# Second block's qkv and attention queries by token from split weights, on one Trainium2 core

## The chip, the cores and the metric

The kernel runs on one core of a Trainium2 chip. The metric is the device time of one execution in microseconds (us), as the median of several runs. The engines are TensorE (PE in the profile, with its weight loads as PEld), VectorE (DVE), ScalarE (ACT), GpSimd (POOL) and SyncE (SP, which here only issues transfers). They run side by side, each along its own queue, and wait for each other by semaphores.

## What is computed

The reference chains two transformer blocks on 256 tokens of width 1024. The first mixes tokens with two gated linear attentions and then sends every token through 8 x 16 experts that are gathered by index. The second block has four branches, whose inputs come from one projection `h @ w_in`; what matters here of it:

```python
h = _rmsnorm(x, norm_pre)
cols = h @ w_in
(dn_qkv, dn_z, dn_b, dn_a, gm_uv, gm_z, sw_q, sw_k, sw_v, sw_z,
 xm_q, xm_z, gate_logits) = _split_cols(cols)
mem_kv = _rmsnorm(mem, norm_mem) @ w_mem_kv
y_a = _deltanet_branch(dn_qkv, dn_z, dn_b, dn_a, conv_w, a_log, dt_bias, dn_norm)
y_b = _spatial_gating_branch(gm_uv, gm_z, gm_norm, spatial_w, spatial_b)
y_c = _sliding_window_branch(sw_q, sw_k, sw_v, sw_z, sinks)
y_m = _memory_branch(xm_q, xm_z, mem_kv)
ys = jnp.stack([y_a, y_b, y_c, y_m], axis=2)
proj = jnp.einsum("btnc,ncd->btnd", ys, w_up)
gates = jax.nn.sigmoid(gate_logits.reshape(B, T, N_BRANCH, D))
merged = jnp.sum(gates * proj, axis=2)
out = merged @ w_out
return x + _rmsnorm(out, norm_post)
```

`dn_qkv` (1536 columns) goes through a causal convolution of four taps along the tokens and a silu; `sw_q` and `xm_q` (512 columns each) are the queries of the two attention branches.

## The kernel before

The 256 tokens are two blocks of 128, b = 0 and 1. The weights lie in HBM as tiles of 128 x 1024 (two chunks of 128 rows by 512 columns), and 512 output columns are a group of four tiles. `load_to` (L205) issues the transfers on SP in the order of the stream, `wt` (L231) calls for a chunk of a tile and keeps the loads ahead.

Products are done in two ways. With float32 operands (`proj_chan` in its second branch, L414) the weights are the stationary operand, the result comes out channel by token, and a chip instruction leaves two records. With split operands (`mm3`, L370) a tile is cut into a high part (a cast on ACT, L216) and a low part (a subtraction on DVE, L217), and three products of 128x512 replace one of full precision: `proj_tok` (L377) for one block, `both_tok` (L391) for both. They come out token by channel. `is_split` and `SPLIT` (L53) say which groups are split; `cut_to` (L219) splits tiles up to `state["ahead"]` tiles before their use, into a ring of six pair buffers.

Block 0 of the second block (`pre2`, `small_proj`, `qkv`, `q_proj`, `deltanet`, L1028 to L1317) runs in the shadow of the expert gathers of block 1: `gathers` (L930) hands a step to the side work between two gathers. After the last gather come `last_out(1)`, the two gm groups (`spatial_u`), and then the tail, in which TensorE follows `tail_main` (L1674). It does, for block 1, the small projection (`swk`), the three qkv groups and the two query groups `swq` and `xmq` channel by token from unsplit weights; after them the four z groups (first `zgm`), the gates and the up products for both blocks, from split weights. Into this order `pace` (L89) sets the steps of four side chains: the delta rule (`tail_delta`, with the products gc, gcr, l2p, l2r), the spatial branch (gmv, sp, yb) and the two attentions (own, prev, sws). `pace` goes by a count of steps, not by durations: a step that is set there waits in its engine's queue until what it needs is ready, and everything behind it on that engine waits too.

For each qkv group, ACT copies the result to `qkvr`, DVE puts the last three tokens of block 0 ahead of it, ACT does the first tap and DVE the other three for each of four channel blocks (L1072, L1074), and a tanh on ACT and one DVE step make the silu.

At the end, `merge(3)` (L1485) adds the last up product into `mg`, block by block, `finish_T` turns `mg` (pt) and `finish` does the out product (o) from the last two split groups.

Of the kernel before, what the change touches and what calls it, by code (L numbers as in the profile page):

```python
# [19 lines left out]
P = 128  # L20
# [26 lines left out]

(G_IN, G_V, G_G, G_OUT, G_Q, G_OUT2, G_MEM, G_QKV, G_SWQ, G_XMQ, Z_GU, Z_GV, G_AGAIN, Z_GZ, Z_SW, Z_XM, Z_DN, G_GATE,
 G_O2, G_END) = (0, 3, 5, 7, 9, 12, 15, 17, 20, 21, 22, 23, 24, 29, 30, 31, 32, 33, 45, 47)
AGAIN = G_AGAIN - G_QKV  # L50
STREAM = (*range(12), 7, 8, *range(12, 22), *range(15, 20), *range(22, 40))

SPLIT = ((G_IN, G_Q), (Z_GU, G_AGAIN), (Z_GZ, G_END))  # L53

UP_B, UP_C, UP_M, UP_A = 0, 1, 2, 3

# [85 lines left out]
def kernel(ctx, tc, I, out, dbg=None):  # L142
    nc = tc.nc
    dbg = dbg or {}
    V, S, G, TE = nc.vector, nc.scalar, nc.gpsimd, nc.tensor
# [10 lines left out]
    def slot(name, dt=F32):  # L156

        return big.tile([P, 1024], dt, tag="slot", name=name)

    def slot3(name, n, w=P, dt=F32):  # L160
        return slot(name, dt)[:, :n * w].rearrange("p (a b) -> p a b", b=w)
# [6 lines left out]
    turn = {"at": 0, "ring": N_PAIR}  # L168
# [114 lines left out]
    def bank4(name, tag="ps"):  # L283
        return bank(name, tag).rearrange("p (a b) -> p a b", b=P)
# [92 lines left out]
    def proj_tok(g, xT, name, n=KC, c0=0, w0=0):  # L377

        ps = bank(name)
        for c in range(n):  # L380
            x = xT(c0 + c)
            if isinstance(x, tuple):
                mm3(ps, x, wt2(g, w0 + c), c == 0, c == n - 1)
            else:
                TE.matmul(ps, x, wt(g, w0 + c), start=c == 0, stop=c == n - 1)
                pe(0.9)
            if c % 2:
                yield
        return ps
# [16 lines left out]
    def proj_chan(ps, g, cb, xT):  # L406

        s = slice(cb * P, (cb + 1) * P)
        for c in range(KC):
            x = xT(c)  # L410
            if isinstance(x, tuple):
                mm3(ps, [w[:, s] for w in wt2(g, c)], x, c == 0, c == KC - 1)
            else:
                TE.matmul(ps, wt(g, c)[:, s], x, start=c == 0, stop=c == KC - 1)  # L414
                pe(0.244)
# [610 lines left out]
    B2 = {}  # L1026
# [16 lines left out]
    def h_of(b):  # L1043
        return lambda c: hT[b][:, c]

    def h2_of(b):
        return lambda c: (hh2[b][0][:, c], hh2[b][1][:, c])

    tail3 = {}

    def qkv(b):

        qkvT = []
        for g in range(3):
            ps = bank("qkv")
            for cb in range(4):
                proj_chan(ps[:, cb * P:(cb + 1) * P], G_QKV + b * AGAIN + g, cb, h_of(b))
                yield
            yield
            raw_ = slot("qkvr")[:, :4 * (P + 3)].rearrange("p (a b) -> p a b", a=4)  # L1060
            S.copy(raw_[:, :, 3:], ps.rearrange("p (a b) -> p a b", a=4))
            if b:
                V.tensor_copy(raw_[:, :, :3], tail3[b - 1, g])
            else:
                V.memset(raw_[:, :, :3], 0.0)
            if b + 1 < NB:
                tail3[b, g] = cpool.tile([P, 4, 3], F32, name=f"tail{b}{g}")
                V.tensor_copy(tail3[b, g], raw_[:, :, P:P + 3])
            dst = slot3(f"qkvT{b}{g}", 4)
            for cb in range(4):  # L1070
                cw = chan[:, C_CW + 4 * (4 * g + cb):C_CW + 4 * (4 * g + cb) + 4]
                S.activation(dst[:, cb], raw_[:, cb, 0:P], AF.Copy, scale=cw[:, 0:1])  # L1072
                for tap in range(1, 4):
                    V.scalar_tensor_tensor(dst[:, cb], raw_[:, cb, tap:tap + P], cw[:, tap:tap + 1],  # L1074
                                           dst[:, cb], op0=OP.mult, op1=OP.add)
                if cb % 2:
                    yield
            th = small("th", 512).rearrange("p (a b) -> p a b", b=P)
            S.activation(th, dst, AF.Tanh, scale=0.5)
            V.scalar_tensor_tensor(dst, th, 1.0, dst, op0=OP.add, op1=OP.mult)  # L1080
            qkvT.append(dst)
            yield
        B2["qkvT", b] = qkvT

    def small_proj(b):

# [12 lines left out]
        B2["swk", b], B2["swv", b], B2["ba", b] = k, v, ba  # L1099
        yield  # L1100

    def q_proj(g, name, b):
        dst = slot3(f"{name}{b}", 4)
        ps = bank(name)
        for j in range(4):
            proj_chan(ps[:, j * P:(j + 1) * P], g + b * AGAIN, j, h_of(b))
            yield
        S.copy(dst, ps.rearrange("p (j t) -> p j t", j=4))
        B2[name, b] = dst

    def z_silu(z, name, gain=None):

        t = B2[name, 0] = slot3(f"{name}_t", 2, 512)
        pss = yield from both_tok(z, (h2_of(0), h2_of(1)), name)
        for b, ps in enumerate(pss):
            dst = t[:, b]
            if gain is not None:
                gate_tok(dst.rearrange("p (h d) -> p h d", h=4), ps, gain)
            else:
                th = small("th", 512)  # L1120
                S.activation(th, ps, AF.Tanh, scale=0.5)
                V.tensor_scalar(th, th, 0.5, 0.5, op0=OP.mult, op1=OP.add)
                V.tensor_tensor(out=dst, in0=th, in1=ps, op=OP.mult)
            B2[name, "of", b] = dst
            yield
# [348 lines left out]
    def gate_proj(n):  # L1474
        for b in range(NB):
            gates[b, n] = slot(f"gate{b}{n}")
        for nh in range(2):
            pss = yield from both_tok(G_GATE + 3 * n + nh, (h2_of(0), h2_of(1)), "gate")
            for b, ps in enumerate(pss):
                S.activation(gates[b, n][:, nh * 512:(nh + 1) * 512], ps, AF.Tanh, scale=0.5)  # L1480
            yield
# [37 lines left out]
    def finish_T(b):  # L1519
        fin[b] = slot3(f"mh{b}", 8, P, F32R), slot3(f"ml{b}", 8, P, F32R)  # L1520

        def put(h, pt):
            hi, lo = [t[:, 4 * h:4 * h + 4] for t in fin[b]]
            S.activation(hi, pt, AF.Copy, scale=0.5)
            V.scalar_tensor_tensor(lo, pt, 0.5, hi.bitcast(F32), op0=OP.mult, op1=OP.subtract)

        yield from transposed(mg[b], put)
# [145 lines left out]

    def tail_main():  # L1674
        yield from small_proj(1)
        yield from qkv(1)
        yield from q_proj(G_SWQ, "swq", 1)
        yield from q_proj(G_XMQ, "xmq", 1)
        yield from z_silu(Z_GZ, "zgm")
        yield from z_silu(Z_SW, "zsw")  # L1680
        yield from z_silu(Z_XM, "zxm")
        yield from z_silu(Z_DN, "zdn", gain=rows[:, R_DN:R_DN + P])
        for n in range(3):
            yield from gate_proj(n)
            yield from merge(n)
        yield from gate_proj(3)
        turned, i = finish_T(0), 0
        for waits in merge(3):
            yield waits
            i += waits is not True  # L1690
            if i > 6:
                next(turned, None)
        yield from turned
# [98 lines left out]
```

## Time and profile before

| what | value |
|---|---|
| median of 3 runs | 1202.18 us (1202.08 to 1202.36) |
| the profiled execution, its time and span | 1201.17 us, 1199.4 us |
| TensorE, busy | 1066.5 us (89%) |
| DVE, busy | 869.9 us (73%) |
| ACT, busy | 508.0 us (42%) |
| splits of tiles: casts on ACT (L216), subtractions on DVE (L217) | 108 of 1052 ns, 108 of 1220 ns |
| 512 float32 products of block 0 and 1 for qkv, records | x384, 275 ns median |

The profile is one execution on the chip. A group of its rows is a line of the kernel, an engine, an operation and a tile, with the busy time and the mean of one. In the views in order of time a row has the start and the time in us, the engine, the line, the operation with output<-inputs and their sizes, how many instructions it merges, and in brackets how long the engine stood idle before it and whom it waited for. The granted clock of TensorE (PEclk) is a share of 2.4 GHz. Times are from the start of the span.

### The profile page before, as it was taken

The numbers are of one execution on the slowest core, as the hardware profiler recorded it, in microseconds if no ns is written. First come the engines' busy times: TensorE is split into PE (matmuls) and PEld (weight loads), VectorE is DVE, ScalarE is ACT, GpSimd is POOL, SyncE is SP. The second block draws the span as 40 slices with busy tenths as digits, with TensorE's granted clock in tenths as the row PEclk, the third lists the DMA queues.
The fourth block names the chain that finished last, engine by engine and source line by source line (L and its number), as shares of the span: only waits on it lengthen the run. The fifth ranks groups of instructions, "written<-read, shape, count | busy, mean of one in ns | idle before, by whom it ended". The sixth has DMA issues, their size and how long they took to land.

```text
span 1199.4 us, 14824 instructions
## 1 busy us (share of the span) xinstructions
PE 1066.5 (89%) x4988; PEld 732.5 (61%) x4988; DVE 869.9 (73%) x1872; ACT 508.0 (42%) x1271; POOL 317.1 (26%) x278
## 2 busy tenths in 40 slices
PE   8999979989979885986888898886999999999987
PEld 6887634545437652733655554543469988888876
DVE  5588587887588667979888899974735686456644
ACT  5625333442343342432444644546534444444441
POOL 1000234334434342543433454552200000000000
PEclk9999989899989997997989989999999999999989
DMA  9626599999999999999999999999753843445520
GB/s 364 220 102 225 209 363 367 355 375 391 427 427 425 425 421 426 425 427 426 406 424 425 403 388 427 426 427 427 288 202 141 300 158 127 127 154 190 191 90 36
DMA packets 68075, 376.40 MB, mean 314 GB/s; under 512 B 7696, under 2 KB 8992, under 8 KB 35232
## 3 DMA queue, kind: packets, MB, share of 16 engines
q0 software_dynamic: 36864, 268.45, 54.4%
q1 hardware_dynamic: 29264, 103.56, 24.2%
q10 hardware_dynamic: 1872, 3.44, 0.8%
q8 instruction: 40, 0.66, 0.2%
q14 instruction: 35, 0.29, 0.1%
HBM read 374.38 MB, written 1.05 MB: 313 GB/s over the span
## 4 chain that ended last, share of the span: by engine, by line
PE 46%; DVE 22%; DMA 15%; issue 7%; ACT 6%; POOL 3%; POOLq 0%; SPq 0%; DVEq 0%; ACTq 0%
DMA uv<-in_peer_uv_dram,idx 12%; PE acc L910 10%; DVE uv L887 8%; POOL uv L858 3%; PE pq L414 3%; PE gate L373 2%; PE gate L375 2%; PE gate L374 2%; DMA w<-in_wts_dram 2%; PE qkv L414 2%; DVE x L904 2%; PE lv L620 2%; DVE wp L217 1%; PE up L373 1%; PE up L374 1%
## 5 line engine op out<-in xcount | busy, mean ns | idle before, releaser
L910 PE MATMUL acc<-uv,dg 128*128 128x512 f32 x852 | 432.3, 644 | 98.5 <-ACT dg L898 93.7
L858 POOL DMA_INDIRECT uv<-in_peer_uv_dram,idx x256 | 303.8, 1187 | 429.5 <-PE acc L910 253.1
L887 DVE SCALAR_TENSOR_TENSOR uv<-uv,hn 128x1024 f32<-128x1024 f32 x256 | 307.9, 1220 | 80.5 <-DMA uv<-in_peer_uv_dram,idx 75.8
L910 PEld LDWEIGHTS acc<-uv,dg 128*128 128x128 f32 x852 | 161.4, 204 | 284.9 <-issue 146.2
L891 ACT ACTIVATE ge<-act 128x1 f32<-128x1 f32 x256 | 51.7, 202 | 376.1 <-DVE uv L887 353.6
L217 DVE TENSOR_TENSOR wp<-w,wp 128x1024 fp32r<-128x1024 f32 x108 | 129.2, 1220 | 74.7 <-ACT wp L216 74.6
L216 ACT CAST wp<-w 128x1024 fp32r<-128x1024 f32 x108 | 110.0, 1052 | 53.8 <-PE up L375 17.7
L898 ACT ACTIVATE dg<-mats,wv 128x128 f32<-128x128 f32 x213 | 82.9, 389 | 4.6 <-PE acc L910 3.1
L295 POOL TENSOR_TENSOR rsb<-rsa,mhalf 128x1 f32<-128x1 f32 (+2 forms) x8 | 7.3, 908 | 283.5 <-DVE rsa L292 283.5
L892 ACT ACTIVATE wv<-ge,gw 128x1 f32<-128x1 f32 x256 | 75.4, 295 | 8.3
L414 PEld LDWEIGHTS pq<-hnT,w 128*128 128x128 f32 x512 | 60.5, 192 | 9.0 <-issue 8.8
L414 PE MATMUL pq<-hnT,w 128*128 128x128 f32 x512 | 61.3, 275 | 0.0
L904 DVE SCALAR_TENSOR_TENSOR x<-uv,wv,x 128x1024 f32<-128x1024 f32 x43 | 55.0, 1280 | 1.9 <-ACT wv L892 1.9
L373 PE MATMUL gate<-wp,hh 128*128 128x512 f32 x128 | 51.7, 404 | 0.0
L414 PEld LDWEIGHTS qkv<-hT,w 128*128 128x128 f32 x384 | 46.4, 196 | 6.8 <-issue 6.6
L375 PE MATMUL gate<-wp,hl 128*128 128x512 f32 x128 | 49.9, 390 | 0.0
L374 PE MATMUL gate<-wp,hh 128*128 128x512 f32 x128 | 49.9, 390 | 0.0
L414 PE MATMUL qkv<-hT,w 128*128 128x128 f32 x384 | 46.4, 279 | 0.0
L323 POOL TENSOR_TENSOR rst<-rst,mhalf 128x1 f32<-128x1 f32 x5 | 2.8, 559 | 146.0 <-DVE rst L322 146.0
L1074 DVE SCALAR_TENSOR_TENSOR qkvT<-qkvr,chan,qkvT 128x128 f32<-128x128 f32 x72 | 24.0, 351 | 5.7 <-ACT qkvT L1072 4.0
L375 PEld LDWEIGHTS gate<-wp,hl 128*128 128x128 f32 x128 | 24.0, 188 | 5.2
L891 ACT ACT_TABLE_LOAD x21 | 26.9, 1283 | 0.4
(503 smaller groups left out, 1780.5 us busy)
## 6 DMA issues: line engine op xcount, KB each, us to landing
w<-in_wts_dram SPq DMA_DIRECT2D x188, 512.0 KB, 4.9
uv<-in_peer_uv_dram,idx POOLq DMA_INDIRECT x256
wsm<-in_w_small_dram ACTq DMA_DIRECT2D x8, 132.0 KB, 9.9
x<-in_x_dram SPq DMA_DIRECT2D x2, 512.0 KB
skT<-in_skT_dram ACTq DMA_DIRECT2D x2, 512.0 KB
mem<-in_mem_dram SPq DMA_DIRECT2D x2, 512.0 KB
out_dram<-o SPq DMA_DIRECT2D x4, 256.0 KB
row_n<-in_gains_dram ACTq DMA_DIRECT2D x1, 512.0 KB
```

The source lines that it names most:

```text
L216: S.copy(hi, x)
L217: (eng or V).tensor_tensor(out=lo, in0=x, in1=hi.bitcast(F32), op=OP.subtract)
L373: TE.matmul(ps, fh, sh, start=start, stop=False)
L374: TE.matmul(ps, fh, sl, start=False, stop=False)
L375: TE.matmul(ps, fl, sh, start=False, stop=stop)
L414: TE.matmul(ps, wt(g, c)[:, s], x, start=c == 0, stop=c == KC - 1)
L858: G.indirect_dma_start(out=t, out_offset=None, in_=I["peer_uv"], in_offset=bass.IndirectOffsetOnAxis(ap=idx[b][:, h, s:s + 1], axis=0))
L887: V.scalar_tensor_tensor(t, t, 1.0, hn[b], op0=OP.mult, op1=OP.mult, accum_out=act[:, h, s:s + 1])
L891: S.activation(ge, act[:, h, s:s + 1], AF.Gelu)
L898: S.activation(dg[diags], ident, AF.Copy, scale=wv[diags])
L904: V.scalar_tensor_tensor(xr[b], t, wv[sums], xr[b], op0=OP.mult, op1=OP.add)
L910: TE.matmul(acc[b][:, nh], dg[sums], t[:, nh * 512:(nh + 1) * 512], start=start, stop=h == 7 and s == 15)
```

## The change

The qkv and query groups of block 1 are now split like the groups after them, so all groups from the gm groups to the end are (`SPLIT`). A new driver, `by_channel`, does each group token by channel with `proj_tok`, copies the result to SBUF (ACT, tile `qkvt`, `swqt` or `xmqt`) and turns it with four transposes (pt) after the second tile of the next group; the last one is turned inside zgm. What followed the products (`qkv_of`, `q_of`) then reads the turned tile. Block 0 keeps its float32 products; its `q_proj` hands on one step more. In the last merge, tiles are split two ahead instead of four. The other lines of the file move by -1 up to L1048 and by up to +41 behind.

```diff
-AGAIN = G_AGAIN - G_QKV
...
-SPLIT = ((G_IN, G_Q), (Z_GU, G_AGAIN), (Z_GZ, G_END))
+SPLIT = ((G_IN, G_Q), (Z_GU, G_END))
...
+    def by_channel(groups, last):
+
+
+        def steps(p):
+            for k, waits in enumerate(p):
+                yield waits
+                if k == 1 and turn:
+                    yield from turned(*turn)
+
+        def turned(t, use):
+            pt = bank4("pt")
+            for c in range(4):
+                TE.transpose(pt[:, c], t[:, c * P:(c + 1) * P], ident)
+            yield
+            yield from use(pt)
+
+        def product(g, name):
+            ps = yield from proj_tok(g, h2_of(1), name)
+            products.append(ps)
+
+        turn, products = None, []
+        for g, name, use in groups:
+            yield from steps(product(g, name))
+            t = slot(f"{name}t")[:, :512]
+            S.copy(t, products.pop())
+            turn = t, use
+        yield from steps(last)
+
...
-                proj_chan(ps[:, cb * P:(cb + 1) * P], G_QKV + b * AGAIN + g, cb, h_of(b))
+                proj_chan(ps[:, cb * P:(cb + 1) * P], G_QKV + g, cb, h_of(b))
                 yield
             yield
+            yield from qkv_of(b, g)(ps.rearrange("p (a b) -> p a b", a=4))
+
+    def qkv_of(b, g):
+        def use(ps):
             raw_ = slot("qkvr")[:, :4 * (P + 3)].rearrange("p (a b) -> p a b", a=4)
-            S.copy(raw_[:, :, 3:], ps.rearrange("p (a b) -> p a b", a=4))
+            S.copy(raw_[:, :, 3:], ps)
...
+    def q_of(name, b):
+        def use(ps):
+            dst = slot3(f"{name}{b}", 4)
+            S.copy(dst, ps)
+            B2[name, b] = dst
+            yield
+
+        return use
+
     def q_proj(g, name, b):
-        dst = slot3(f"{name}{b}", 4)
         ps = bank(name)
         for j in range(4):
-            proj_chan(ps[:, j * P:(j + 1) * P], g + b * AGAIN, j, h_of(b))
-            yield
-        S.copy(dst, ps.rearrange("p (j t) -> p j t", j=4))
-        B2[name, b] = dst
+            proj_chan(ps[:, j * P:(j + 1) * P], g, j, h_of(b))
+            yield
+        yield from q_of(name, b)(ps.rearrange("p (j t) -> p j t", j=4))
...
         yield from small_proj(1)
-        yield from qkv(1)
-        yield from q_proj(G_SWQ, "swq", 1)
-        yield from q_proj(G_XMQ, "xmq", 1)
-        yield from z_silu(Z_GZ, "zgm")
+        yield from by_channel([(G_AGAIN + g, "qkv", qkv_of(1, g)) for g in range(3)]
+                              + [(G_AGAIN + 3, "swq", q_of("swq", 1)), (G_AGAIN + 4, "xmq", q_of("xmq", 1))],
+                              z_silu(Z_GZ, "zgm"))
...
         yield from gate_proj(3)
+        state["ahead"] = 2
```

How the queues change shows at three places. The names are those of the tiles with the number of their buffer; wp and a number is a split tile of the stream, 96 to 99 that of qkv group 0, 100 to 103 of group 1, and so on by fours to 112 to 115 of xmq; th, dd and dg_r belong to the silu of a group and to the decay gates.

ACT, before, from the end of the decay gates' first step to the copy of group 1:

```order
L1139 ACTIVATE dg_r_6508<-ba_6496 128x4
L1061 COPY qkvr_6554<-qkv_6510 128x4x128 [waits PE_49]
L1072 ACTIVATE qkvT10_6557<-qkvr_6554,chan_78 128x128 [waits DVE_49]
L1072 ACTIVATE qkvT10_6557<-qkvr_6554,chan_78 128x128 x3
L1079 ACTIVATE th_6584<-qkvT10_6557 128x512 [waits DVE_49]
L1154 ACTIVATE dg_r_6508<-dg_r_6508 128x4 [waits DVE_49]
L1155 ACTIVATE dg_r_6508<-dg_r_6508 128x4 [waits DVE_49]
L1162 ACTIVATE dd_6609<-dd_6609 128x512 [waits DVE_49]
L1163 ACTIVATE dd_6609<-dd_6609 128x512 [waits DVE_49]
L1061 COPY qkvr_6657<-qkv_6587 128x4x128 [waits PE_49]
```

ACT, in the change, behind the copy of group 0 out of PSUM (qkvt) and up to that of group 1:

```order
L215 CAST wp104_6572<-w104_6534 128x1024 [waits DMAHW1_49]
L215 CAST wp105_6586<-w105_6545 128x1024 [waits DMAHW2_49]
L1091 COPY qkvr_6610<-pt_6595 128x4x128 [waits PE_49]
L1102 ACTIVATE qkvT10_6613<-qkvr_6610,chan_78 128x128 [waits DVE_49]
L1102 ACTIVATE qkvT10_6613<-qkvr_6610,chan_78 128x128 x3
...
L1196 ACTIVATE dg_r_6520<-dg_r_6520 128x4 [waits DVE_49]
L1203 ACTIVATE dd_6635<-dd_6635 128x512 [waits DVE_49]
L1204 ACTIVATE dd_6635<-dd_6635 128x512 [waits DVE_49]
L1109 ACTIVATE th_6646<-qkvT10_6613 128x512
L215 CAST wp106_6651<-w106_6556 128x1024 [waits DMAHW3_49]
L215 CAST wp107_6665<-w107_6570 128x1024 [waits DMAHW4_49]
L1074 COPY qkvt_6674<-qkv_6569 128x512 [waits PE_49]
```

Between the first taps of group 0 and the copy of group 1 now stand the decay gates' steps, the tanh of group 0 and the casts of 106 and 107; the copy of group 1 before stood behind the exponentials alone and fed the taps directly.

TensorE, in the change, from the end of tile 104 (group 2) to tile 106; before, the products of group 2 had no operation of their own group between them:

```order
L374 MATMUL qkv_6676<-wp104_6572,hl1_6338 128x512
L1399 MATMUL sp_6688<-gmv_6405,swT_3159 128x128 [waits DVE_49,Activation_49]
L1399 MATMUL sp_6688<-gmv_6405,swT_3159 128x128 x3
L1399 MATMUL sp_6693<-gmv_6405,swT_3159 128x128 [waits DVE_49]
L1399 MATMUL sp_6693<-gmv_6405,swT_3159 128x128 x3
L372 MATMUL qkv_6676<-wp105_6586,hh1_6337 128x512
L373 MATMUL qkv_6676<-wp105_6586,hh1_6337 128x512
L374 MATMUL qkv_6676<-wp105_6586,hl1_6338 128x512
...
L1062 MATMUL pt_6709<-mats_77,qkvt_6674 128x128 [waits DVE_49,Activation_49]
L1062 MATMUL pt_6709<-mats_77,qkvt_6674 128x128 x3
L372 MATMUL qkv_6676<-wp106_6651,hh1_6337 128x512
L373 MATMUL qkv_6676<-wp106_6651,hh1_6337 128x512 [waits DVE_49]
```

The transposes of group 1 stand between the second and the third tile of group 2, and all tiles behind them wait with them.

DVE, before, in the last merge (gate and mg of the two halves of block 0 and the first of block 1):

```order
L217 TENSOR_TENSOR wp180_8397<-w180_8341,wp180_8397 128x1024 [waits DMAHW5_49,PE_49,Activation_49]
L217 TENSOR_TENSOR wp181_8408<-w181_8358,wp181_8408 128x1024 [waits DMAHW6_49,PE_49,Activation_49]
L1498 SCALAR_TENSOR_TENSOR gate03_8249<-gate03_8249,up_8394 128x512 [waits PE_49]
L1499 TENSOR_TENSOR mg0_7661<-mg0_7661,gate03_8249 128x512 [waits DVE_49]
L217 TENSOR_TENSOR wp182_8422<-w182_8375,wp182_8422 128x1024 [waits DMAHW7_49,Activation_49]
L217 TENSOR_TENSOR wp183_8433<-w183_8395,wp183_8433 128x1024 [waits DMAHW0_49,Activation_49]
L1498 SCALAR_TENSOR_TENSOR gate03_8249<-gate03_8249,up_8419 128x512
L1499 TENSOR_TENSOR mg0_7661<-mg0_7661,gate03_8249 128x512 [waits DVE_49]
L1525 SCALAR_TENSOR_TENSOR ml0_8452<-pt_8453,mh0_8451 128x512 [waits Activation_49]
L1498 SCALAR_TENSOR_TENSOR gate13_8250<-gate13_8250,up_8444 128x512
L1499 TENSOR_TENSOR mg1_7663<-mg1_7663,gate13_8250 128x512 [waits DVE_49]
```

and in the change:

```order
L1539 SCALAR_TENSOR_TENSOR gate03_8304<-gate03_8304,up_8449 128x512 [waits PE_49]
L1540 TENSOR_TENSOR mg0_7721<-mg0_7721,gate03_8304 128x512 [waits DVE_49]
L216 TENSOR_TENSOR wp180_8471<-w180_8396,wp180_8471 128x1024 [waits DMAHW5_49,Activation_49]
L216 TENSOR_TENSOR wp181_8482<-w181_8413,wp181_8482 128x1024 [waits DMAHW6_49,Activation_49]
L1539 SCALAR_TENSOR_TENSOR gate03_8304<-gate03_8304,up_8468 128x512 [waits PE_49]
L1540 TENSOR_TENSOR mg0_7721<-mg0_7721,gate03_8304 128x512 [waits DVE_49]
L1566 SCALAR_TENSOR_TENSOR ml0_8501<-pt_8502,mh0_8500 128x512 [waits Activation_49]
L1539 SCALAR_TENSOR_TENSOR gate13_8305<-gate13_8305,up_8493 128x512 [waits PE_49]
L1540 TENSOR_TENSOR mg1_7723<-mg1_7723,gate13_8305 128x512 [waits DVE_49]
L1566 SCALAR_TENSOR_TENSOR ml0_8501<-pt_8515,mh0_8500 128x512 [waits Activation_49]
L1539 SCALAR_TENSOR_TENSOR gate13_8305<-gate13_8305,up_8524 128x512 [waits PE_49]
L1540 TENSOR_TENSOR mg1_7723<-mg1_7723,gate13_8305 128x512 [waits DVE_49]
```

The subtractions of 182 and 183 have moved from ahead of the second half of mg0 to behind both halves of mg1.

## Rows read from the trace of the kernel before

**Rows 1.** Windows: stretch, length, busy PE, PEld, DVE, ACT, POOL, PEclk, DMA, GB/s.

```profile
900.00:920.00 20.00, 20.00 (x170) 19.61 (x170) 6.86 (x24) 9.40 (x20) 1.10 (x2) 1.00 0.30 106
920.00:940.00 20.00, 20.00 (x182) 20.00 (x181) 15.66 (x51) 8.04 (x20) 0.00 (x0) 1.00 0.73 254
940.00:960.00 20.00, 20.00 (x137) 18.16 (x137) 11.45 (x15) 10.59 (x20) 1.65 (x1) 1.00 0.88 305
960.00:980.00 20.00, 19.49 (x112) 16.55 (x111) 17.95 (x31) 10.13 (x21) 0.00 (x0) 1.00 0.54 179
```

**Rows 2.** TensorE in order of time, 891 to 951 us: start, time, operation.

```profile
891.20 0.39 PE L373 MATMUL gm<-wp,hh 128*128 128x512 f32 x1
...
896.64 0.39 PE L373 MATMUL gm<-wp,hh 128*128 128x512 f32 x1
...
905.72 7.31 PE L414 MATMUL qkv<-hT,w 128*128 128x128 f32 x64
912.86 0.28 PE L1146 MATMUL gc<-dg_g,mats 128*128 128x4 f32 x2
...
914.20 7.31 PE L414 MATMUL qkv<-hT,w 128*128 128x128 f32 x64
...
940.99 1.16 PE L1376 MATMUL own<-swk,swq 64*128 64x128 f32 x8
...
942.97 3.84 PE L414 MATMUL xmq<-hT,w 128*128 128x128 f32 x32
...
950.52 0.48 PE L373 MATMUL zgm<-wp,hh 128*128 128x512 f32 x1
```

**Rows 3.** TensorE in order of time, the tail.

```profile
1158.28 0.60 PE L350 MATMUL pt<-mats,mg 128*128 128x128 f32 x4
1158.63 0.48 PE L373 MATMUL up<-wp,yT 128*128 128x512 f32 x1
...
1164.08 1.08 PE L350 MATMUL pt<-mats,mg 128*128 128x128 f32 x4 [3.81 <-DVE mg L1499]
1164.81 0.78 PE L373 MATMUL up<-wp,yT 128*128 128x512 f32 x1
...
1169.91 0.40 PE L373 MATMUL o<-wp,mh 128*128 128x512 f32 x1
```

**Rows 4.** ACT in order of time, 887 to 923 us.

```profile
887.18 3.90 ACT L216 CAST wp<-w 128x1024 fp32r<-128x1024 f32 x4
...
910.89 0.20 ACT L1139 ACTIVATE dg_r<-ba 128x4 f32<-128x4 f32 x1
...
922.67 0.63 ACT L1162 ACTIVATE dd<-dd 128x512 f32<-128x512 f32 x1 [1.67 <-DVE dd L1160]
```

**Rows 5.** DVE in order of time: the last gathers, the stretch, the tail.

```profile
815.35 1.23 DVE L887 SCALAR_TENSOR_TENSOR uv<-uv,hn 128x1024 f32<-128x1024 f32 x1 [1.21 <-DMA uv<-in_peer_uv_dram,idx]
...
888.26 4.63 DVE L217 TENSOR_TENSOR wp<-w,wp 128x1024 fp32r<-128x1024 f32 x4 [0.26 <-ACT wp L216]
903.51 0.15 DVE L292 TENSOR_SCALAR rsa<-ss 128x1 f32<-128x1 f32 x1 [10.63 <-ACT th L316]
...
913.68 0.17 DVE L1063 COPY qkvr<-tail 128x12 f32<-128x12 f32 x1 [2.39 <-ACT qkvr L1061]
...
918.48 1.41 DVE L1354 SCALAR_TENSOR_TENSOR gmv<-gmv,rsb,row_gm 128x512 f32<-128x512 f32 x2
...
920.41 0.15 DVE L1152 COPY dg_r<-gc 128x4 f32<-128x4 f32 x1
...
922.81 0.15 DVE L1165 SCALAR_TENSOR_TENSOR dg_r<-dg_r 128x4 f32<-128x4 f32 x1
...
929.33 2.15 DVE L1362 SCALAR_TENSOR_TENSOR yb<-sp,chan,gmu 128x128 f32<-128x128 f32 x8
...
1159.55 1.22 DVE L217 TENSOR_TENSOR wp<-w,wp 128x1024 fp32r<-128x1024 f32 x1 [2.63 <-ACT wp L216]
```

**Rows 6.** Windows, TensorE alone, in the tail: busy, PEclk, DMA, GB/s.

```profile
1166.00:1170.00 4.00, 4.00 (x12) 0.54 0.00 0
```

More of the change, by code (lines that the diff above doesn't have):

```diff
@@ L1049 @@
     tail3 = {}
+    def by_channel(groups, last):
[20 more added lines that the diff above has]
+        yield from steps(last)
     def qkv(b):
-        qkvT = []
         for g in range(3):
@@ L1080, in qkv @@
             V.scalar_tensor_tensor(dst, th, 1.0, dst, op0=OP.add, op1=OP.mult)
-            qkvT.append(dst)
+            three = B2.setdefault(("qkv", b), [])
+            three.append(dst)
+            if len(three) == 3:
+                B2["qkvT", b] = three
             yield
-        B2["qkvT", b] = qkvT
+        return use
     def small_proj(b):
@@ L1100, in small_proj @@
         yield
+    def q_of(name, b):
[4 more added lines that the diff above has]
+            yield
+        return use
     def q_proj(g, name, b):
-        dst = slot3(f"{name}{b}", 4)
         ps = bank(name)
         for j in range(4):
-            proj_chan(ps[:, j * P:(j + 1) * P], g + b * AGAIN, j, h_of(b))
+            proj_chan(ps[:, j * P:(j + 1) * P], g, j, h_of(b))
             yield
-        S.copy(dst, ps.rearrange("p (j t) -> p j t", j=4))
-        B2[name, b] = dst
+        yield from q_of(name, b)(ps.rearrange("p (j t) -> p j t", j=4))
     def z_silu(z, name, gain=None):
```

## The prediction

> **What bounds the kernel now.** I read the windows first, then the instructions of TensorE, VectorE (DVE) and ScalarE (ACT) in order of time. Between 900 and 960 us TensorE is busy 20.00 us of every 20 at a granted clock of 1.00, while DVE has 6.86, 15.66 and 11.45 us [rows 1]. So the stretch that the change rewrites, from the small projection at 902 us to the first z product at 950.52 us [rows 2], is bound by TensorE, and DVE seems to have room. That room is the question: what counts is not its sum but its place in the queues of DVE and ACT, each of which runs its instructions in the order in which they stand.
>
> **TensorE's part.** A group is now 32 full-precision products of 128x128 (64 records); the first one starts at 905.72 and what follows it at 912.86, 7.14 us [rows 2]. In the change a group is 24 products of 128x512 with split weights; the two token products of gm start at 891.20 and 896.64, so 24 of these take 5.44 us, 1.36 us a tile [rows 2]. Behind each group come four transposes, which in the tail take 0.35 us, with 0.09 us more for the first product behind them [rows 3]: 0.45 us. Five groups go from 35.7 to 29.45 us: 6.25 us less work for TensorE.
>
> **ACT's and DVE's part.** The 20 tiles of these groups have to be split: a cast on ACT, four in 3.90 us, 0.975 us each [rows 4], and a subtraction on DVE, four in 4.63 us, 1.16 us each [rows 5]. That adds 19.5 us to ACT and 23.2 us to DVE, and ACT gets five more copies of 128x512 out of PSUM, at 0.6 us like the other ACT steps of that size (0.63 us [rows 4]). The first four tiles fit into a hole of 10.63 us on DVE before 903.51 [rows 5] and cost nothing. The other sixteen stand among the rest. I walk through them on the clock of the profile before.
>
> Start. ACT has three table loads behind the small projection and is free at 911.1 [rows 4]. Only then come the casts of tiles 100 to 103, done at 912.1 to 915.0; the subtractions of 100 to 104 follow to 917.9, and behind them the two small steps of the decay gates, to 918.3. TensorE ends group 0 at 911.16, does tiles 100 and 101 and the first transposes to 916.2, then stands at the product gc, which needs those small steps: 2.1 us. With gc at 1.34 us (912.86 to 914.20 [rows 2]), tiles 102 to 104, the product sp (sixteen records, as own and prev have together: 1.98 us) and tile 105 it comes to 927.05.
>
> First long wait. Next on TensorE are the transposes of group 1, whose copy stands on ACT behind the casts of 106 and 107, these behind the tanh of group 0 and two exponentials, and these behind DVE's work on group 0. From 918.3: a small step and the subtraction of 105, 1.4; the two gmv products, 1.41; the convolution of a group from its tail copy to its last tap, 4.80 (913.68 to 918.48); the gate differences, 2.40 (920.41 to 922.81) [rows 5]; three ACT steps of about 0.6 [rows 4], 1.7; two casts, 1.95; the copy, 0.6. Sum 14.3: 932.6. TensorE waits 5.5 us.
>
> Second long wait. It then does transposes, tiles 106 to 109 (0.4 us late for one subtraction) and stands at 938.9 before the transposes of group 2. DVE: subtraction 106 ends at 932.2, a small step and two products, 1.6; subtractions 107 to 109, 3.5; the yb products, 2.15; the convolution, 4.80 [rows 5]: 944.2. ACT: tanh 0.6, two casts, the copy: 947.4. TensorE waits 8.5 us.
>
> Third wait. After tiles 110 to 113 TensorE is at 953.3. Subtraction 110 ends at 947.0, 111 to 113 at 950.4, the convolution at 955.2; ACT's tanh and two squares end at 957.0 (l2p can start, 3.7 us late), casts 114 and 115 at 959.0, the copy of swq at 959.6, casts 116 and 117 and the copy of the turned swq at 962.1. Only then come the scores own and prev, 1.98 us (940.99 to 942.97 [rows 2]), tiles 114 and 115, 2.72, and own and prev once more: zgm starts at 968.8 instead of 950.52 [rows 2]. So the stretch costs **18.3 us more**, the 6.25 us of TensorE's saving already in it. Behind 960 us TensorE was busy 19.49 of 20 [rows 1] with the same work as in the change, so nothing takes the delay back.
>
> What of it is not seen in a row: how the queues of DVE and ACT mesh. If all sixteen splits hid, the stretch would gain 6.25 us; if every one of them lay bare on DVE, sixteen times 1.16 us would cost 18.6 us less the 6.25. The chain above comes out beyond the second bound by about 6 us, because ACT and DVE also wait for each other, so I take the chain and use both ends in the cases below. The weights' transfers stay hidden: a raw buffer is now free after the subtraction instead of after the products, and the DMA engines are busy 0.30 to 0.88 of the stretch [rows 1].
>
> **The tail.** With the split-ahead set to 2, the splits of tiles 182 and 183 stand behind the sums of mg0 and mg1. Before, DVE waited for their casts (the first came at 1159.55, after 2.63 us [rows 5]) and added mg0 only behind both; TensorE stood 3.81 us for it and then ran slower: its twelve up products that start at 1164.81 end where the next product starts, at 1169.91, 5.1 us instead of 12 times 0.227 (5.44 / 24) [rows 3]. In that stretch the granted clock was 0.54, its lower level of 1.2 GHz [rows 6]. In the change the second half of mg0 needs only the up half that ends 1.36 us before 1158.28 [rows 3] and two DVE steps on 128x512 (two took 1.41 us [rows 5]), so it is there at about 1159.5, before the transposes are due at 1160.1. From 1160.1 to the out product 9.8 us become 0.36 + 2.72 + 0.1 = 3.2 us: **6.6 us less**. The later splits (182 to 187) are then due at one in 1.36 us, against 0.975 us on ACT and 1.16 on DVE. Bounds: 0, if one of them holds TensorE as mg0 did, and 6.6.
>
> **The gathers.** q_proj hands on one step more in block 0, which moves the side work behind the gathers by one gather. The wait of DVE for a gather in that place was 1.21 us [rows 5]; one gather more or less in front of the ACT-bound end is worth between -1.2 and +2.5 us (one gather and its dot, 1.23 + 1.21). I take **+0.5**.
>
> **Sum.** 18.3 - 6.6 + 0.5 = +12.2 us. The profiled execution took 1201.17 us for a span of 1199.4; the median of the runs is 1202.18, 1.01 above. So 1202.18 + 12.2 = **1214.4 us**.
>
> **Rivals.**
> (1) Faster: TensorE stays the bound. If ACT and DVE stay ahead of it, as the free sums of 13.1, 4.3 and 8.6 us of DVE in the three windows allow on paper [rows 1], both savings come: 1202.18 - 6.25 - 6.6 + 0.5 = 1189.8 us. The Trainium skill's Perfetto Trace Analysis, "Identifying the Most-Contended Engine", says to optimize the engine with the highest occupancy first; by that rule, with TensorE at 20.00 of 20, this is the case to expect. Against it: the copy that feeds the transposes stands behind two casts and the whole convolution of the group before, whatever the sums are. It decides for this case if the copy of group 1 ends before 927 us. Chance 0.08.
> (2) No change: the waits come, but half as long, since the stages mesh better than I add them up. 18.3 would have to shrink to about 6, with the tail's 6.6 against it: 1202.2 us. Chance 0.05.
> (3) Slower than forecast: the clock. After each of the three waits TensorE starts at its lower level, as after the 3.81 us in the tail, where the restart cost 5.1 - 2.72 = 2.4 us, and 0.4 more in the transposes, 1.08 instead of 0.60 [rows 3]. Behind the first and the second wait this lies under the next wait; if it does not, or lasts into zgm, three times 2.7 us come on top: 1222.5 us. The Trainium skill's TensorE: Matmul & The Clock Gate, "HAM oscillation", states that waits between bursts of products bring the clock down each time; by that rule this is the time. The tail's wait agrees (0.54), but no row here shows a wait that another wait follows. Chance 0.10.
> (4) The tail does not do what it says: tile 182 or 186 holds TensorE instead of mg0, and the 6.6 us stay: 1221.0 us. Chance 0.05.
>
> **Numbers.** That leaves 0.72 for the forecast, whose own range is 1207 to 1220: the gathers move it by 2 and each of the three chains by some 2 us. The range 1206 to 1222 takes in case 4 and part of case 3 and leaves out about 2 in 10. A measurement of this kernel tells some 0.2%, 2.4 us, from no change. Slower by more: 0.72 + 0.10 + 0.05 = 0.87; within: 0.05; faster: 0.08.
>
> **What would show it.** In the profile of the changed kernel: zgm starts 17 to 20 us later against the small projection; TensorE has idle times of about 5, 8 and 4 us before the transposes pt of groups 1 and 2 and before l2p, released by ACT copies named qkvt; the granted clock falls between 925 and 965 us; the 3.81 us wait for mg is gone, and from the last gate product to the end there are about 6.6 us less. It would be wrong if the copies qkvt end within a microsecond of their products, if TensorE stays busy through to zgm, or if the tail keeps a wait of over 2 us.

## Result: 1212.8 us, slower by 1%

The changed kernel takes 1212.8 us in the median (1212.25 to 1214.6, 4 runs), the kernel before 1202.13 us (4 runs); the ratio is 1.0097 with a 95% interval of 1.0085 to 1.0109. The forecast was 1214.4 us in a range of 1206 to 1222. The profiled execution of the change has a span of 1211.2 us, 11.8 more than before.

The windows of the changed kernel (the columns are those of [rows 1], to which they answer):

```profile
900.00:920.00 20.00, 16.84 (x92) 13.93 (x92) 11.15 (x23) 14.06 (x25) 1.10 (x2) 1.00 0.52 186
920.00:940.00 20.00, 13.15 (x54) 10.31 (x52) 17.31 (x47) 8.11 (x16) 0.00 (x0) 0.83 0.33 108
940.00:960.00 20.00, 13.98 (x59) 11.62 (x60) 16.34 (x26) 15.23 (x23) 1.32 (x1) 0.70 0.51 162
960.00:980.00 20.00, 20.00 (x97) 16.64 (x97) 9.90 (x14) 8.96 (x25) 1.27 (x1) 0.87 0.51 178
```

TensorE, 20.00 of 20 before, is busy 13 to 14 of 20 from 920 to 960 us, and its granted clock falls to 0.83 and 0.70 in the two windows. TensorE in order of time, the changed kernel (answers to [rows 2]):

```profile
899.03 1.95 PE L1124 MATMUL swk<-hT,wsm 128*128 128x128 f32 x16
...
912.93 0.60 PE L1062 MATMUL pt<-mats,qkvt 128*128 128x128 f32 x4
915.19 0.36 PE L1187 MATMUL gc<-dg_g,mats 128*128 128x4 f32 x2 [1.66 <-DVE dg_r L1184]
...
928.63 1.12 PE L1062 MATMUL pt<-mats,qkvt 128*128 128x128 f32 x4 [3.40 <-ACT qkvt L1074]
...
943.04 1.12 PE L1062 MATMUL pt<-mats,qkvt 128*128 128x128 f32 x4 [5.55 <-ACT qkvt L1074]
...
952.36 1.95 PE L1224 MATMUL l2p<-one,X 128*128 128x1 f32 x16 [0.78 <-ACT X L1219]
...
957.61 2.08 PE L1417 MATMUL own<-swk,swq 64*128 64x128 f32 x8 [1.26 <-ACT swq L1139]
...
968.06 0.50 PE L372 MATMUL zgm<-wp,hh 128*128 128x512 f32 x1
```

The waits stand where the forecast put them, before the transposes of groups 1 and 2, and their releaser is the copy qkvt on ACT. From swk to zgm it is 69.03 us instead of 48.44 (902.08, the start of swk before, to 950.52). That is 20.6 us more, a little beyond the 17 to 20 us that the forecast named as its sign. ACT in order of time shows what the copies stand behind, the tanh of the group before and two casts:

```profile
925.61 0.61 ACT L1109 ACTIVATE th<-qkvT 128x512 f32<-128x512 f32 x1
926.12 1.97 ACT L215 CAST wp<-w 128x1024 fp32r<-128x1024 f32 x2
928.01 0.57 ACT L1074 COPY qkvt<-qkv 128x512 f32<-128x512 f32 x1
...
935.28 1.28 ACT L1102 ACTIVATE qkvT<-qkvr,chan 128x128 f32<-128x128 f32 x4 [4.31 <-DVE qkvr L1093]
939.99 0.63 ACT L1109 ACTIVATE th<-qkvT 128x512 f32<-128x512 f32 x1 [3.43 <-DVE qkvT L1104]
940.53 1.98 ACT L215 CAST wp<-w 128x1024 fp32r<-128x1024 f32 x2
942.41 0.58 ACT L1074 COPY qkvt<-qkv 128x512 f32<-128x512 f32 x1
```

And the tail on TensorE (answers to [rows 3]): both transposes of mg come without a wait, and from the first to the out product it is 5.03 us instead of 11.63.

```profile
1176.37 0.60 PE L349 MATMUL pt<-mats,mg 128*128 128x128 f32 x4
...
1178.21 0.60 PE L349 MATMUL pt<-mats,mg 128*128 128x128 f32 x4
...
1181.40 0.39 PE L372 MATMUL o<-wp,mh 128*128 128x512 f32 x1
```

The 11.8 us by places: up to swk -3.05, swk to zgm +20.59, zgm to the first transposes of mg +0.55, from there to the out product -6.60, behind it +0.31.

### The profile page after: what moved, and what is told of

Read it like the earlier page. It is cut to its first block, busy times and chain, and to the rows that moved or that the text cites. A ratio compares the mean times of both kernels' runs of the same rounds, so it can differ in the third digit from the quotient of the medians.

```text
span 1211.2 us, 14536 instructions
## 1 busy us (share of the span) xinstructions
PE 1066.9 (88%) x4808; PEld 726.2 (60%) x4808; DVE 893.2 (74%) x1892; ACT 526.3 (43%) x1294; POOL 320.7 (26%) x278
## 4 chain that ended last, share of the span: by engine, by line
PE 39%; DVE 25%; DMA 18%; issue 8%; ACT 6%; POOL 4%; SPq 0%; POOLq 0%; ACTq 0%; DVEq 0%
DMA uv<-in_peer_uv_dram,idx 14%; DVE uv L886 9%; PE acc L909 7%; POOL uv L857 4%; PE gate L372 2%; PE gate L374 2%; PE gate L373 2%; PE pq L413 2%; DMA w<-in_wts_dram 2%; DVE x L903 2%; DVE qkvT L1104 2%; PE lv L619 1%; DVE wp L216 1%; PE up L372 1%; PE up L374 1%
## 5 line engine op out<-in xcount | busy, mean ns | idle before, releaser
L216 DVE TENSOR_TENSOR wp<-w,wp 128x1024 fp32r<-128x1024 f32 x128 | 152.1, 1220 | 74.6 <-ACT wp L215 74.3
L215 ACT CAST wp<-w 128x1024 fp32r<-128x1024 f32 x128 | 129.2, 1049 | 47.4 <-PE gate L374 10.7
L413 PEld LDWEIGHTS qkv<-hT,w 128*128 128x128 f32 x192 | 25.1, 204 | 6.8 <-issue 6.4
L372 PEld LDWEIGHTS gate<-wp,hh 128*128 128x128 f32 x128 | 24.1, 188 | 4.6
L373 PEld LDWEIGHTS gate<-wp,hh 128*128 128x128 f32 x128 | 24.1, 188 | 4.6
```

The source lines that it names most:

```text
L215: S.copy(hi, x)
L216: (eng or V).tensor_tensor(out=lo, in0=x, in1=hi.bitcast(F32), op=OP.subtract)
L372: TE.matmul(ps, fh, sh, start=start, stop=False)
L373: TE.matmul(ps, fh, sl, start=False, stop=False)
```

## The experiments

Two theories stood against each other for the 20.6 us. **Place**: what TensorE waits for stands on ACT behind the silu of the group before. **Sum**: DVE cannot do 23.2 us more in that stretch, wherever it stands. A third, the **clock**, was rival 3. The ratios are to the kernel before, measured on the same chip. Where two versions are compared in us, their medians are; they come from several chips, on which the kernel before took 1201.1 to 1202.1 us, and by the ratios a difference can come out up to 2 us larger or smaller.

### The tail and the gathers apart

`tail_alone`, the kernel before with one line:

```diff
         yield from gate_proj(3)
+        state["ahead"] = 2
```

> The kernel before with one line more: the split-ahead is set to 2 behind the last gate product. If the order of the last splits alone makes the tail, the 3.81 us wait of TensorE for mg and the stretch at half clock behind it vanish, and the kernel takes 6.0 to 6.6 us less than before (about 1195.8 us). If the tail of the changed kernel gained because everything came some 18 us later and the splits had time to get ahead, this line alone gives nothing (1202 us) and a wait for mg or for a split tile stays in the trace.

Measured: 1195.39 us against 1201.55, ratio 0.9947 (0.9930 to 0.9964), 6.2 us less. The wait for mg is gone. The line alone makes the tail. The reverse is `no_tail`, the changed kernel without that line:

> The changed kernel without the line that sets the split-ahead to 2 behind the last gate product; the front is as in the change. If the tail is worth there what it is worth alone, the wait of TensorE for mg is back and the kernel takes 6.0 to 7.3 us more than the changed one, about 1219.5 us, with 157.5 us from the first gate product to the first out product instead of 150.6. If the late start of the gates gives the splits more room there, the time stays at 1213 us.

Measured: 1219.54 us, ratio 1.0169 (1.0143 to 1.0195), 6.7 us above the change (8.7 by the ratios). TensorE in order of time, `no_tail`:

```profile
1177.55 0.60 PE L349 MATMUL pt<-mats,mg 128*128 128x128 f32 x4
...
1183.35 0.63 PE L349 MATMUL pt<-mats,mg 128*128 128x128 f32 x4 [3.81 <-DVE mg L1540]
...
1188.14 0.41 PE L372 MATMUL o<-wp,mh 128*128 128x512 f32 x1
```

The wait for mg is back, and from the first transposes to the out product it is 10.59 us instead of 5.03. So the tail and the front add up, within some 2 us.

`yield_alone`, the kernel before with the additional step:

```diff
         B2[name, b] = dst
+        if not b:
+            yield
```

> The kernel before with one step more handed on by q_proj in block 0, as in the change; everything else as before. If this step is what moved the end of the gathers, the small projection swk starts about 3 us earlier than before (899.0 against 902.1 us) and the kernel takes about 3 us less (1199 us). If the 3 us of the changed kernel are the scatter of the gathers from one execution to the next, nothing moves: 1202 us, and swk starts at 902 within 1 us.

Measured: 1199.97 us, ratio 0.9986 (0.9973 to 0.9999). Neither number came out: half of the 3 us by the median, and in its profile swk starts at 903.64, later than before. `tail_yield` has both lines:

> The kernel before with the two parts of the change that are not splits: the step that q_proj hands on in block 0, and the split-ahead of 2 in the last merge. If both add up, 1202 - 6.2 - 1.6 = about 1194 us; if the step in the gathers is scatter, 1195.5 to 1196 us, as with the tail line alone.

Measured: 1192.91 us against 1201.13, ratio 0.9943 (0.9923 to 0.9964), the fastest version of this study. By the ratios the step adds 0.0004 to the tail line's gain, alone 0.0014: between nothing and 2 us. In the profiles of the kernels with this step swk starts anywhere from 897.0 to 903.6, so most of the 3.05 us is scatter of the gathers, and what the step is worth stays open.

### Sum or place

`lag2` asks for each copy one group later:

```diff
-                if k == 1 and turn:
-                    yield from turned(*turn)
+                if k == 1 and len(turn) > 1 or last_ and k == 3:
+                    yield from turned(*turn.pop(0))
```

> The changed kernel with each group turned one group later: the transposes stand behind the second tile of the group after next, so a copy out of PSUM has 5.44 us more before it is asked for; the work is the same. If the place of the copies decides, the waits before the transposes (3.40 and 5.55 us), before swq's (0.94) and before own (1.26) go and with them the stretches at half clock (about 11 us lost): some 18 to 20 us less than the changed kernel, 1193 to 1195 us. If the sum of VectorE's work decides (48 us of it between the small projection and zgm, against 38 us of products on TensorE), the waits only move to the split tiles wp: about 8 to 10 us less, 1203 to 1205 us, with TensorE waiting for VectorE's wp.

Measured: 1214.75 us, ratio 1.0125 (1.0101 to 1.0150): no gain; from swk to the first gate product it is 131.9 us, in the change 131.8. TensorE in order of time, `lag2`:

```profile
928.66 0.60 PE L1062 MATMUL pt<-mats,qkvt 128*128 128x128 f32 x4
...
932.98 0.80 PE L372 MATMUL swq<-wp,hh 128*128 128x512 f32 x1 [3.72 <-ACT wp L215]
...
942.42 0.60 PE L1062 MATMUL pt<-mats,qkvt 128*128 128x128 f32 x4
...
946.10 0.53 PE L372 MATMUL xmq<-wp,hh 128*128 128x512 f32 x1 [3.08 <-ACT wp L215]
```

The transposes no longer wait, but a split tile now does in their place, and its releaser is again ACT: its cast. That spoke for the sum, or for casts that stand as badly as the copies. `no_sub` tells these apart, the changed kernel without the new subtractions:

```diff
+                if 4 * G_AGAIN <= i < 4 * G_AGAIN + 20:
+                    S.copy(hi, raw[i])
+                    lo = hi
```

> The changed kernel without the 20 new subtractions on VectorE (the low part of these tiles is the high part again, so this part of the product is left out); the casts, the copies and the order of everything else stay. If VectorE's added work is the bound, 20 times 1.16 us go and TensorE becomes the bound of the stretch: from the small projection to zgm some 44 to 47 us instead of 69.0, the kernel 22 us or more below the changed one, 1188 to 1191 us. If the place of the copies on ScalarE, behind casts and tanh, is what costs, the waits before the transposes keep over half of their 3.40 and 5.55 us and the kernel stays above 1200 us.

Measured: 1205.64 us, ratio 1.0035 (1.0020 to 1.0050), 7.2 us below the change and not 22. From swk to zgm it is 61.65 us instead of 69.03. TensorE and ACT in order of time, `no_sub`:

```profile
927.69 0.66 PE L1066 MATMUL pt<-mats,qkvt 128*128 128x128 f32 x4 [3.41 <-ACT qkvt L1078]
...
938.01 1.11 PE L1066 MATMUL pt<-mats,qkvt 128*128 128x128 f32 x4 [4.17 <-ACT qkvt L1078]
```

```profile
927.54 1.99 ACT L227 CAST wp<-w 128x1024 fp32r<-128x1024 f32 x2
929.43 0.58 ACT L1095 COPY qkvr<-pt 128x512 f32<-128x512 f32 x1
930.26 1.28 ACT L1106 ACTIVATE qkvT<-qkvr,chan 128x128 f32<-128x128 f32 x4 [0.24 <-DVE qkvr L1097]
934.96 0.63 ACT L1113 ACTIVATE th<-qkvT 128x512 f32<-128x512 f32 x1 [3.42 <-DVE qkvT L1108]
935.50 1.97 ACT L227 CAST wp<-w 128x1024 fp32r<-128x1024 f32 x2
937.38 0.58 ACT L1078 COPY qkvt<-qkv 128x512 f32<-128x512 f32 x1
```

With 23 us less on DVE both waits stand, 3.41 us as before and 4.17 of 5.55. This is a round: copy of the turned group, first taps, 3.42 us in which ACT waits for DVE's taps, tanh, two casts, copy of the next group, its transposes, two casts, and again a copy of a turned group. It takes 10.3 us (927.69 to 938.01), although neither engine is full in it (in these 10.32 us DVE is busy 6.47 and ACT 6.65); TensorE needs 5.9 us for a group (5.44 and 0.45). In the change, with subtractions in it, the round takes 14.4 us (928.63 to 943.04), and there DVE is nearly full, 12.72 of 14.41 us. The difference shows in one wait: before the first taps ACT stands 4.31 us for DVE, where the tail copy (L1093) stands behind three subtractions more, and 0.24 us here. So the subtractions lengthen the round, but it stays too long without them.

`lag2_no_sub` takes away both:

> Both ceilings taken away at once: each group is turned one group later and the 20 new subtractions on VectorE are left out (the low part is the high part again, so that part of the product is left out). If the changed kernel stands between two ceilings, the round from copy to copy through the convolution (10.3 us a group without subtractions) and VectorE's work for a group (4.24 + 0.69 + 0.17 + 4 times 1.16 = 9.7 us), both above TensorE's 5.9 us, then either one alone leaves the other, and only both together let TensorE through: from the small projection to the first gate product 109 to 113 us as in the kernel before, instead of 131.8, and some 1190 us in all. If the two runs that took away one of them show two parts that simply add up (7 us from the subtractions, 0 from the later turn), it is 1205 us again.

Measured: 1206.97 us, ratio 1.0061 (1.0037 to 1.0085). From swk to the first gate product it is 120.3 us in its profile: 11.5 less than in the change, but not 109 to 113. That profile is the fastest of the four runs (1202.70 us), and by the medians the later turn adds nothing to `no_sub`, 1206.97 against 1205.64 us, as the other branch of the expectation had it (1205 us). The expectation that both together let TensorE through is refuted. TensorE and ACT in order of time:

```profile
936.75 0.50 PE L376 MATMUL xmq<-wp,hh 128*128 128x512 f32 x1 [4.15 <-ACT wp L227]
...
947.49 2.66 PE L1228 MATMUL l2p<-one,X 128*128 128x1 f32 x14 [3.40 <-ACT X L1223]
```

```profile
935.13 0.63 ACT L1113 ACTIVATE th<-qkvT 128x512 f32<-128x512 f32 x1 [3.42 <-DVE qkvT L1108]
935.67 1.98 ACT L227 CAST wp<-w 128x1024 fp32r<-128x1024 f32 x2
```

The round is unbroken (ACT's tanh at 924.80, 935.13 and 946.29): the casts of the next tiles stand in it just as the copies do. So place it is, in a wider sense than in the forecast: not the copy alone but all that ACT does for TensorE stands behind the tanh, hence behind DVE's taps. A version that also takes the casts out of the round was not tried; that TensorE would then come through is argued from these rows, not shown.

`pool_sub` puts every second subtraction on GpSimd:

```diff
-                cut(raw[i], hi, lo, eng or V)
+                cut(raw[i], hi, lo, eng or (G if 4 * G_AGAIN <= i < 4 * G_AGAIN + 20 and i % 2 else V))
```

> The changed kernel with the subtraction of every second one of the 20 new tiles on GpSimd instead of VectorE: ten times 1.16 us leave VectorE. If the place in the queues decides, only the subtractions that stand in the three chains before a copy count (105; 107 and 109; 111 and 113): about 5 us less than the changed kernel, with waits before the transposes of groups 1 and 2 still over 2 us each. If the sum of VectorE's work decides, 11.6 us less. If GpSimd needs more than about 2.7 us for a subtraction (two tiles of TensorE's time), TensorE waits for wp from GpSimd instead and the gain is smaller than 5 or turns into a loss.

Measured: 1221.52 us, ratio 1.0159 (1.0139 to 1.0179), 9 us above the change; the branch of the slow GpSimd came, a loss. GpSimd and VectorE in order of time:

```profile
901.34 2.38 POOL L216 TENSOR_TENSOR wp<-w,wp 128x1024 fp32r<-128x1024 f32 x1 [4.25 <-ACT wp L215]
...
913.69 9.08 POOL L216 TENSOR_TENSOR wp<-w,wp 128x1024 fp32r<-128x1024 f32 x3 [8.13 <-ACT wp L215]
```

```profile
914.59 5.98 DVE L216 TENSOR_TENSOR wp<-w,wp 128x1024 fp32r<-128x1024 f32 x2 [0.67 <-ACT wp L215]
920.49 2.29 DVE L1182 SCALAR_TENSOR_TENSOR dg_g<-dg_z,dg_g 128x4 f32<-128x4 f32 x1
```

Three subtractions on GpSimd take 3.0 us each (one at 901.34, with DVE idle, 2.38 us), and in that time two on DVE take 3.0 us each instead of 1.16, and a step on 128x4 takes 2.29 us instead of 0.16. DVE is not relieved but held, so this run does not decide between sum and place.

### The clock

`fill` lets TensorE work through the two long waits (12 and 20 products that nobody reads):

```diff
             pt = bank4("pt")
+            for _ in range(n):
+                TE.matmul(pt.rearrange("p a b -> p (a b)"), h2_of(1)(0)[0], hh2[0][0][:, :4].rearrange("p a b -> p (a b)"), start=True, stop=True)
```

> The changed kernel with products that nobody reads ahead of the transposes of groups 1 and 2 (12 and 20 of 128x512, 2.7 and 4.5 us at full clock), which fill the waits of 3.40 and 5.55 us, so that TensorE does not fall to its lower level there. If the clock costs time on the path, the 5.4 us lost at half clock behind these two waits come back: about 5 us less than the changed kernel. If VectorE sets the pace, the time stays within 1.5 us of the changed kernel: TensorE is faster behind the transposes and then stands longer at the next place, with the copies at the same times.

Measured: 1215.18 us, ratio 1.0121 (1.0105 to 1.0138): no gain, 2.4 us above the change by the median, and in the profiles the same span (1211.1 and 1211.2 us). TensorE in order of time:

```profile
925.15 2.88 PE L1062 MATMUL pt<-hh,hh 128*128 128x512 f32 x12
928.72 0.65 PE L1064 MATMUL pt<-mats,qkvt 128*128 128x128 f32 x4 [0.70 <-ACT qkvt L1076]
...
934.98 4.69 PE L1062 MATMUL pt<-hh,hh 128*128 128x512 f32 x20
943.12 0.66 PE L1064 MATMUL pt<-mats,qkvt 128*128 128x128 f32 x4 [3.45 <-ACT qkvt L1076]
...
952.45 3.57 PE L1226 MATMUL l2p<-one,X 128*128 128x1 f32 x16 [3.19 <-ACT X L1221]
```

The transposes take 0.65 us instead of 1.12, so TensorE is at its upper level; and they start 29.6 and 44.0 us after swk, as in the change (29.6 and 44.0). What TensorE saves there it stands at l2p, 3.19 us instead of 0.78. The lower clock behind the first two waits costs nothing: the round sets the time.

### Fewer groups, another order

`q_only` splits swq and xmq alone, `tail_xmq` xmq alone; both have the tail line and the step in block 0.

> The changed kernel with the three qkv groups of block 1 back in full precision and only the two query groups swq and xmq split and turned: 8 tiles to split instead of 20, none of them beside the first two convolutions. TensorE's work falls by 2 times (7.14 - 5.44 - 0.45) = 2.5 us. If VectorE has room for 9.3 us in the 60 us from the small projection to 960 us (34 of 60 busy before), the kernel comes out 2.5 us below the kernel before with the tail line alone: about 1193 us. If swq's copy or the splits stand behind the convolution of group 2 (4.8 us) and the tanh, TensorE waits 3 to 6 us before swq's transposes or at a split tile, and the time is 1196 to 1199 us.

> The two parts that are not splits, and of the five groups only the last, xmq, split and turned: four tiles, whose casts come while TensorE still does swq, and a copy that no convolution stands ahead of. If TensorE's saving shows where neither ceiling is touched, 7.14 - 5.44 - 0.45 = 1.25 us less than with the two parts alone, 1193 to 1194 us. If the four subtractions (4.6 us) push the convolution of group 2 and with it l2p, TensorE waits there 2 to 4 us: 1195 to 1198 us.

Measured: `q_only` 1202.3 us, ratio 1.0006 (0.9995 to 1.0017); `tail_xmq` 1200.24 us, ratio 0.9997 (0.9981 to 1.0012). That is 9 and 7 us above `tail_yield` (7.6 and 6.5 by the ratios) where 2.5 and 1.25 us less work was to show, and beyond the slower branch of either expectation. From swk to zgm it is 56.57 and 54.66 us instead of 48.44. In `q_only` l2p waits 3.87 us and the first tile of swq 0.63 and 1.71. ACT and TensorE in order of time, `tail_xmq`:

```profile
933.41 3.87 ACT L215 CAST wp<-w 128x1024 fp32r<-128x1024 f32 x4
937.18 0.57 ACT L1139 COPY swq<-swq 128x512 f32<-128x512 f32 x1
```

```profile
937.81 2.07 PE L1417 MATMUL own<-swk,swq 64*128 64x128 f32 x8 [2.83 <-ACT swq L1139]
```

The casts of only four tiles, behind the last tanh and the two squares, hold the copy of swq by 3.8 us, and TensorE comes out of the wait at its lower level (own 2.07 us instead of 1.16). One group is enough, and here without the round of the groups: four casts ahead of one copy do it.

`mix` takes the groups in the order qkv 0, swq, qkv 1, xmq, qkv 2:

> The changed kernel with the groups in the order qkv 0, swq, qkv 1, xmq, qkv 2 (the weights come in the same order), all else as in the change. VectorE has the same work, but a convolution now falls into every second group, and the last one (4.9 us with its silu) moves behind the start of zgm. If the sum of VectorE's work up to zgm decides, the gain is that one convolution, 5 us (1208 us). If the convolution of the group ahead of each copy decides, two of the long waits go and it is 10 us or more (1203 us or less). If the last convolution then holds TensorE at l2p in zgm, nothing is gained.

Measured: 1220.52 us, ratio 1.0149 (1.0125 to 1.0174). No expectation held: own waits 4.53 us for yb on DVE, and the transposes of xmq 5.73 us for a copy. Other products come forward and wait in the same queues.

## Why the prediction was right, and where it was off

- **The stretch, +18.3, measured +20.6.** The mechanism stands: the walk through the two queues gives the releasers and, counted from swk, the copy of group 1 at 30.5 us (measured 29.6), that of group 2 at 45.3 (44.0), l2p at 54.9 (53.3), own at 60.0 (58.6). Each came 0.9 to 1.6 us earlier than forecast, 0.9 of it from the first chain. Only the end is later than forecast, zgm at 69.0 instead of 66.7: the step "own and prev, tiles 114 and 115, own and prev" was reckoned at full clock, 6.68 us, and took 10.45 (957.61 to 968.06). That is the term of the stretch that was too small: TensorE has no wait in it, but its granted clock is 0.50 from 956 to 964 us.
- **The waits were shorter than forecast** (3.40, 5.55, 0.78 us against 5.5, 8.5, 3.7), with five small ones of 0.75 to 1.26 us beside them (the walk does not list these; its times leave room for all but the 0.94 us before the second half of sp). TensorE came 1.2 to 1.6 us later to each of the three: to the first because of the small waits, at full clock, to the second also because it ran at its lower level behind the first. Waits and clock are one loss here, shared out differently.
- **Rival 3, the clock**, happened in part: of the 8.1 us put on it 3.8 lie on the path, behind the last wait, where no further wait hides them; the first two cost nothing (`fill`). The Trainium skill's TensorE: Matmul & The Clock Gate, "HAM oscillation", states that waits between bursts bring the clock down; the trace agrees for the two long ones (0.50 from 928 to 932 and from 944 to 948 us). The third drop, the one that costs, followed no long wait, only short ones of 0.78, 0.94 and 1.26 us around l2p. What a drop costs depends on what ends last behind it.
- **Rival 1**, TensorE as the bound, fell: what decided is a round through two engines, busy 17 and 8 of 20 us (DVE and ACT from 920 to 940). The copy of group 1 came 29.6 us after swk, where this rival needed it before 24.9 (927 on the clock of the profile before). By the rule of the Trainium skill's Perfetto Trace Analysis, "Identifying the Most-Contended Engine", one would have cut TensorE's work; the page judges TensorE's headroom by its rate of arithmetic and its weight loads, not by the busy time of its products, but the weight loads too were 18.16 to 20.00 of 20 us [rows 1]. Here that work was cut, and the kernel became slower.
- **The second bound** of the forecast, every subtraction bare on DVE, was the wrong yardstick: the subtractions are worth 7 us (`no_sub`); the rest is read from the rows as place and clock.
- **The tail, -6.6**: measured -6.60 in the profile; -6.2 alone.
- **The gathers, +0.5**: -3.05 in this profile, by medians between 0 and -2. The sign was chosen badly, and most of it is scatter.

The sum is close (12.2 against 11.8 in the profile) because two errors cancel: 2.3 us too little for the stretch, 3.5 too much for the gathers (and 0.9 us elsewhere). That the sum is this close is luck; that the kernel came out slower, and by which waits, is not.

## What to carry to other kernels

Before moving work from a full engine to two with room, draw the round that the new work closes: from a result on TensorE through ACT, DVE and ACT back to what TensorE needs next. If that round takes longer than TensorE's share of it (here 14.4 us, and 10.3 without the subtractions, against 5.9), the free sums in the windows do not tell the time. What one engine does for another that is ahead of it (copies, casts) must not stand behind a step that waits for a third; and a small line that only reorders splits (6 us here) should be measured apart from the large change that carries it.

## What the runs showed of the hardware beyond that

GpSimd and VectorE hold each other up: see the rows of `pool_sub`, 2.29 us for a step of 0.16. The Trainium skill's SBUF — State Buffer, "SBUF: two separate sides", states that the two share a port pair as an exclusive lock, held for a whole instruction; the trace agrees with that.

The clock can fall without any wait. Windows of TensorE alone in `tail_alone` (busy, PEclk, DMA share, GB/s), which has the same products there as the kernel before, and the last row of its own products:

```profile
936.00:940.00 4.00, 4.00 (x39) 1.00 0.78 249
940.00:944.00 4.00, 4.00 (x26) 0.73 0.92 336
944.00:948.00 4.00, 4.00 (x21) 0.50 0.95 287
```

```profile
938.78 1.84 PE L1183 MATMUL l2p<-one,X 128*128 128x1 f32 x16
...
943.11 6.48 PE L414 MATMUL xmq<-hT,w 128*128 128x128 f32 x32
```

TensorE is busy all the time, yet behind l2p (16 records of one column each) and the scores own the clock goes to 0.50, and the 32 records of xmq take 6.48 us instead of 3.84 [rows 2]. In the profile before, and in those of `yield_alone` and `tail_yield`, the same products take 3.84 us there, so l2p alone does not bring it. What does stays open; it is one of the things by which executions of the same products differ.
